# A two-layer encoder trunk: GpSimd left idle in the first pair, the shift earlier, and layer norm as two VectorE operations

## The chip, the cores and the metric

The kernel runs on one core of a Trainium2 chip. The metric is the device time of one execution in microseconds (us), as a median over runs. The engines are named as in the profile: PE is TensorE's matmul and PEld its weight load, DVE is VectorE, ACT is ScalarE, POOL is GpSimd, SP is SyncE, which here issues most of the DMAs. Each engine works through its own queue in order and waits on semaphores for the others.

## The reference

Two groups of tokens, p (1024 tokens) and s (512), go through the same two layers of width 1024. Cut to what matters here:

```python
for l in range(2):
    mod = silu(c) @ w_mod[l] + b_mod[l]
    shift, scale, gate = split(mod, 3)
    u = x * (1 + scale) + shift
    y = mixer_a(u, w_in_a, w_out_a) if l == 0 else mixer_b(u, w_in_b, w_out_b, sink_b)
    x = layernorm(ALPHA * x + gate * y, ln_g[l], ln_b[l])
# layernorm(h) = (h - mean) * rsqrt(var + 1e-5) * g + b, over the 1024 columns
```

mixer_a projects u to q, k and v for three dilations (1, 4 and 16) and to a gate z, runs windowed attention for each dilation, merges them and multiplies by w_out. mixer_b is windowed attention with grouped keys. All inputs and results are float32.

## The kernel before

*Accuracy and chunks.* A float32 product is made of three faster ones. Every operand is split into hi (a rounded copy, type fp32r) and lo (operand minus hi), and each step over 128 rows of the contraction is three matmuls: hi of the weight with hi of u, hi with lo, lo with hi. With eight such steps a group of 512 columns is 24 matmuls (`run_plan`, L370, into the PSUM tiles `a`, of which there are two). The work is a list of chunks, each with one or two weight tiles of 128x1024, one or more groups and an evacuation of the PSUM tile (L160 on ScalarE, L162 on VectorE).

*Order.* The program is written out in the order in which each engine shall work; nothing is reordered later. While a group's matmuls are written, `slot()` is called after every four of them (eight where they have 256 columns) and after each evacuation. `after(n, f)` writes the work of f at the n-th slot from there, `spread(tasks, slots)` lets a list of tasks follow slot by slot, with None for an empty slot, and `hook(i, f)` writes f ahead of chunk i. A slot later in the program is a place later in every queue that f uses.

*Weights.* `w_load` (L316) brings a tile from DRAM on SP's queue, two tiles ahead. `w_split` makes hi and lo of the next tile. The chunk's `how` says where: "pool" makes both on GpSimd (hi in two halves, L336; lo in four quarters, L346), "act" makes hi on ScalarE (L338) and lo on GpSimd, "fast" makes hi on ScalarE and lo in one operation on VectorE. Buffers in SBUF are 45 slabs of 128x1024 words, given and returned by hand.

*The start.* The first layer for s comes first. A pair is the work of two heads; the first pair's chunks 0 to 3 make q4, k4, q16 and k16, chunk 4 the values of dilations 4 and 16 (four groups of 24 matmuls with 256 columns). x of s is transposed into xT (L1346). Of the three parts of `mod`, scale is computed first (`mod_mm`, L206, then `mod_tr`: L212, L218, L220, and L227/L228 on VectorE), so chunks 0 to 3 can start on u without shift: `u_scaled` makes hi on ScalarE (L1315) and lo on VectorE (L1316). The shift is computed between them, from the weights `mods[1]` (eight loads). Then `whole` makes u with shift (`u_whole`: the sum for even k on ScalarE, L1325, for odd k on VectorE, L1321; hi at L1326 and L1322; lo on GpSimd, L1327, and VectorE, L1323), and `swap` puts it in place ahead of chunk 4 (EARLY is 4). What chunks 0 to 3 lack, `early_bias` adds: VectorE accumulates shift times the weight over k (`acc`, L1295 and L1297, 16 operations for two weight tiles), TensorE sums over the partitions with ones (L1304), and VectorE adds the column to Q4, K4, Q16 and K16 (L1306, L1309). The first scores are L578.

*Out layers and layer norm.* After both groups' attention, w_out is applied in 12 blocks of 128 tokens, each of two groups of 24 matmuls; this happens once in each layer. A block's evacuation on VectorE multiplies by the gate (L1093, tile ystg), adds ALPHA x (L1094) and takes the statistics of the half (L1095). Then follow, by slots: `stat` (mean and variance on VectorE, L1105; on GpSimd minus the mean, plus eps, to the power -0.5, and their product, L1106 to L1109), four slots after it `norm` on ScalarE (L1113, x times rstd minus mean times rstd), two later `scale` (times g, L1117), three later `shift` (plus b, L1121), and the store (L1123, SP). Of each block one of scale and shift is on VectorE and the other on GpSimd, alternating by block. The last block of all is done in halves at once (`finish_last`). Other work shares the engines there: L736, L794, L804 and L805 merge the last attention results, L787 reads back their factors f_p, L1069 and L1070 split the next block's input, L275 and L278 transpose x of s for the second layer, whose first steps are L946 and L949.

Of the kernel before, what the change touches and what calls it, by code (L numbers as in the profile page):

```python
# [75 lines left out]
def trunk(ctx: ExitStack, tc: tile.TileContext, x_p, x_s, c_p, c_s, w_mod, b_mod, ln_g, ln_b,  # L76
# [248 lines left out]
    def w_split():  # L325
        i = ahead[1]
        if i < len(loads):
            ahead[1] += 1
            t = raw_t.pop(i)
            hi = slabs.get(F32R, t.shape)  # L330
            lo = slabs.get(F32R, t.shape)
            how = loads[i][1]
            k = t.shape[1]
            if how == "pool":
                for ks in (slice(0, k // 2), slice(k // 2, k)):
                        nc.gpsimd.tensor_scalar(hi[:, ks], t[:, ks], 1.0, 1.0, ALU.mult, ALU.mult)  # L336
            else:
                nc.scalar.activation(hi, t, AF.Copy)  # L338
            if i == 0:
                for k in (0, 4):  # L340
                    nc.gpsimd.tensor_tensor(lo[:, k:k + 4], t[:, k:k + 4], hi[:, k:k + 4].bitcast(F32), ALU.subtract)
            else:
                n = 1 if how == "fast" else 4
                f = lambda a, j: a.rearrange("p k c -> p (k c)")[:, D // n * j:D // n * (j + 1)]
                for j in range(n):
                    (nc.vector if how == "fast" else nc.gpsimd).tensor_tensor(  # L346
                        f(lo, j), f(t, j), f(hi, j).bitcast(F32), ALU.subtract)
            if i < EARLY:
                early[i] = t
            else:  # L350
                slabs.put(t)
            w_t[i] = (hi, lo)
            w_fetch()
# [467 lines left out]
    def layer_a(r, half=None, done=None, use=None):  # L821
# [6 lines left out]
        for p in range(NP):  # L828
# [86 lines left out]
            if early_p:  # L915
# [3 lines left out]
                  how="act" if r == "s" else "pool")  # L919
# [126 lines left out]
    class Block:  # L1046
# [54 lines left out]
        def stat(self):  # L1101
            P = nc.gpsimd
            self.mv = mv = wk.tile([128, 2], F32, tag="mv", name="mv", bufs=4)
            self.nm = nm = wk.tile([128, 1], F32, tag="nmr", name="nmr", bufs=4)
# [3 lines left out]
            P.tensor_tensor(mv[:, 1:2], mv[:, 1:2], mhalf, ALU.pow)  # L1108
            P.tensor_tensor(nm, nm, mv[:, 1:2], ALU.mult)  # L1109

        def norm(self, cs=slice(0, D)):
            x = self.x[:, cs]
            nc.scalar.activation(x, x, AF.Identity, bias=self.nm, scale=self.mv[:, 1:2])  # L1113

        def scale(self, engine, cs=slice(0, D)):
            x = self.x[:, cs]
            engine.tensor_tensor(x, x, ROW["g"][:, cs], ALU.mult)  # L1117

        def shift(self, engine, cs=slice(0, D)):
            x = self.x[:, cs]  # L1120
            engine.tensor_tensor(x, x, ROW["b"][:, cs], ALU.add)  # L1121
# [6 lines left out]
        def finish(self):  # L1128

            V, P = nc.vector, nc.gpsimd  # L1130
            e = (V, P) if self.b % 2 else (P, V)
            keep = (self.r, self.l) == ("s", 0)
            return [self.stat, None, None, None, self.norm, None, lambda: self.scale(e[0]), None, None,
                    lambda: self.shift(e[1])] + ([] if keep else [self.free])

        def finish_last(self):
            V, P = nc.vector, nc.gpsimd
            self.stat()
            parts = [slice(0, 512), slice(512, 1024)]
            for cs in parts:  # L1140
                self.norm(cs)
            for cs in parts:
                self.scale(V, cs)
                self.shift(V, cs)
            self.free()

    def out_layer(l, first, p0):
# [22 lines left out]
        def then(j):  # L1170
            def f():
# [11 lines left out]
                t = [None] * (8 if j == 0 else 1) + t  # L1183
# [24 lines left out]
    with tc.manual_schedule():  # L1208
# [109 lines left out]
        def u_whole(k, t, m, u):  # L1318
            hi, lo = u[:, 0], u[:, 1]
            if k % 2:  # L1320
                nc.vector.tensor_scalar(t, t, m[:, 8 + k:9 + k], m[:, k:k + 1], ALU.mult, ALU.add)  # L1321
                nc.vector.tensor_copy(hi, t)  # L1322
                nc.vector.tensor_tensor(lo, t, hi.bitcast(F32), ALU.subtract)  # L1323
            else:
                nc.scalar.activation(t, t, AF.Identity, bias=m[:, k:k + 1], scale=m[:, 8 + k:9 + k])  # L1325
                nc.scalar.activation(hi, t, AF.Copy)  # L1326
                nc.gpsimd.tensor_tensor(lo, t, hi.bitcast(F32), ALU.subtract)  # L1327
# [37 lines left out]
        def whole():  # L1365
            for k in range(NK):
                new.append(slabs.get(F32R, (128, 2, 512)))
                u_whole(k, xk[k], m, new[k])
            slabs.put(*xT)
# [47 lines left out]
```

## Time and profile before

| | us |
|---|---|
| median of 3 runs | 2642.94 |
| lowest and highest | 2630.94, 2643.33 |
| the profiled execution | 2628.36 |
| its span, first to last instruction | 2626.3 |
| mean granted TensorE clock | 0.992 of full |

The profile is of one execution, so its numbers are summed against 2628.36 and not against the median. In its tables a row of a stage gives the busy time of each engine with the number of instructions in brackets, then PEclk (the granted TensorE clock as a share of full speed), the DMA engines' busy share and GB/s. In the timeline a row gives start and duration, engine, source line, operation, tiles written and read with their shapes, the number of instructions joined, and in square brackets the idle time of that engine before it with what ended it. Idle time of an engine that nothing waits for costs nothing.

### The profile page before, as it was taken

What the parts mean: (1) busy time and instruction counts of PE and PEld (TensorE: products, weight loads), DVE (VectorE), ACT (ScalarE), POOL (GpSimd) and SP (SyncE); (2) the same over time, 40 slices, a digit from 0 to 9 for tenths busy, and PEclk for the clock granted to TensorE, in tenths of its full rate; (3) what the DMA queues carried; (4) which work ended last, traced back from release to release, by engine and by line L of the source; (5) the groups of instructions that cost most, each with busy time, mean ns of one, the idle gap of its engine ahead of it and who ended that gap; (6) DMA issues with size and microseconds to landing.
All of it is one profiled execution on the core that took longest, in us unless ns stands there. A gap on an engine that the chain in (4) does not pass through costs nothing.

```text
span 2626.3 us, 39811 instructions
## 1 busy us (share of the span) xinstructions
PE 2565.7 (98%) x15139; PEld 2117.3 (81%) x15139; DVE 1114.8 (42%) x2602; ACT 981.8 (37%) x2327; POOL 1073.3 (41%) x1495
## 2 busy tenths in 40 slices
PE   7999999999999999999999999998999999999998
PEld 5777778888888888888888888887787778888786
DVE  4533333333243424333333434245654553454666
ACT  3344345643142424233232424232326643444421
POOL 5343444445323424332324233226546752233633
PEclk9999999999999999999999999999999999999999
DMA  8454543333222212132323232225442320112453
GB/s 283 122 136 143 154 100 106 101 101 91 61 58 70 68 48 67 41 81 58 81 51 79 49 81 58 61 68 172 158 155 66 101 85 25 49 49 65 137 176 112
DMA packets 294678, 247.38 MB, mean 94 GB/s; under 512 B 29656, under 2 KB 257880, under 8 KB 294488
## 3 DMA queue, kind: packets, MB, share of 16 engines
q1 hardware_dynamic: 291160, 244.35, 32.8%
q8 instruction: 119, 1.95, 0.3%
q10 hardware_dynamic: 3328, 0.49, 0.1%
q14 instruction: 71, 0.58, 0.1%
HBM read 198.16 MB, written 25.67 MB: 85 GB/s over the span
## 4 chain that ended last, share of the span: by engine, by line
PE 72%; DVE 2%; ACT 1%; POOL 1%; DMA 1%; issue 1%; SPq 0%; POOLq 0%; DVEq 0%; ACTq 0%
PE a L370 56%; PE o L475 5%; PE t L434 5%; PE s L573 2%; PE s L574 2%; PE s L578 1%; POOL s L269 0%; PE t L591 0%; DMA s<-g_s 0%; DVE s L1094 0%; ACT P L423 0%; ACT ustg L278 0%; DMA s<-s 0%; DVE s L1121 0%; DMA s<-in_x_sample_dram 0%
## 5 line engine op out<-in xcount | busy, mean ns | idle before, releaser
L370 PE MATMUL a<-s,s 128*128 128x512 f32 (+1 forms) x9648 | 2113.0, 369 | 14.0 <-DVE ystg L1093 5.2
L370 PEld LDWEIGHTS a<-s,s 128*128 128x128 f32 x9648 | 1613.7, 190 | 294.5 <-issue 16.5
L346 POOL TENSOR_TENSOR s<-s,s 128x256 fp32r<-128x256 f32 x844 | 618.9, 767 | 469.6 <-PE a L370 203.1
L423 ACT ACTIVATE P<-P,st 128x256 f32<-128x256 f32 (+2 forms) x576 | 312.5, 543 | 559.3 <-DVE st L417 557.6
L417 DVE CUSTOM_DVE_ANT_0 P<-s,bias 128x256 f32<-128x256 f32 (+2 forms) x576 | 251.5, 473 | 270.9 <-PE s L578 130.0
L336 POOL TENSOR_SCALAR s<-s 128x512 fp32r<-128x512 f32 x278 | 171.2, 635 | 408.9 <-PE a L370 346.0
L444 DVE COPY PT<-t 128x256 f32<-128x256 f32 (+3 forms) x320 | 141.4, 449 | 170.1 <-PE t L434 166.5
L736 POOL TENSOR_TENSOR s<-s,s 128x256 f32<-128x256 f32 x92 | 66.7, 753 | 339.0 <-DMA s<-f_p 282.8
L434 PE MATMUL t<-ident,P 128*128 128x128 f32 x1408 | 201.2, 273 | 0.8 <-ACT PT L442 0.8
L434 PEld LDWEIGHTS t<-ident,P 128*128 128x128 f32 x1408 | 168.6, 139 | 29.4 <-ACT PT L442 1.2
L549 DVE TENSOR_TENSOR s<-a,s 64x512 fp32r<-64x512 f32 x128 | 110.0, 860 | 164.1 <-ACT s L547 163.1
L475 PE MATMUL o<-PT,s 128*64 128x256 f32 (+1 forms) x1984 | 178.7, 324 | 0.0
L442 ACT ACTIVATE PT<-t 128x256 f32<-128x256 f32 (+3 forms) x320 | 126.6, 400 | 127.6 <-PE t L434 125.5
L475 PEld LDWEIGHTS o<-PT,s 128*64 128x64 f32 x1984 | 119.1, 136 | 64.7 <-issue 33.8
L573 PE MATMUL s<-s,s 128*128 128x256 f32 (+2 forms) x512 | 144.9, 299 | 10.3 <-DVE st L417 10.2
L574 PE MATMUL s<-s,s 128*128 128x256 f32 (+2 forms) x512 | 143.5, 297 | 2.5 <-DMA s<-s 2.5
L162 DVE COPY s<-a 128x128 f32<-128x128 f32 (+2 forms) x113 | 53.5, 492 | 213.3 <-PE a L370 200.2
L558 DVE TENSOR_TENSOR s<-a,s 64x512 fp32r<-64x512 f32 x80 | 77.5, 969 | 143.9 <-ACT s L556 142.9
L160 ACT ACTIVATE s<-a 128x128 f32<-128x128 f32 (+2 forms) x139 | 52.9, 409 | 224.4 <-PE a L370 224.4
L573 PEld LDWEIGHTS s<-s,s 128*128 128x128 f32 x512 | 97.1, 190 | 25.2 <-DVE st L417 15.8
L547 ACT ACTIVATE s<-a 64x512 fp32r<-64x512 f32 x128 | 100.2, 783 | 25.6 <-PE a L370 24.8
L584 DVE SCALAR_TENSOR_TENSOR s<-th,a 128x512 f32<-128x512 f32 x48 | 43.1, 899 | 151.9 <-ACT th L582 151.9
(112 smaller groups left out, 1573.5 us busy)
## 6 DMA issues: line engine op xcount, KB each, us to landing
s<-in_w_in_a_dram SPq DMA_DIRECT2D x128, 512.0 KB, 5.3
s<-in_w_mod_dram SPq DMA_DIRECT2D x48, 512.0 KB, 7.9
s<-in_w_in_b_dram SPq DMA_DIRECT2D x40, 512.0 KB, 5.2
s<-in_w_in_a_dram SPq DMA_DIRECT2D x64, 256.0 KB, 3.3
s<-s SPq DMA_DIRECT2D x64, 256.0 KB, 5.2
s<-f_p SPq DMA_DIRECT2D x48, 256.0 KB, 5.1
s<-in_x_prompt_dram SPq DMA_DIRECT2D x16, 512.0 KB, 4.2
g_p<-s SPq DMA_DIRECT2D x16, 512.0 KB, 2.6
```

What stands on the lines that cost most here:

```text
L336: nc.gpsimd.tensor_scalar(hi[:, ks], t[:, ks], 1.0, 1.0, ALU.mult, ALU.mult)
L346: (nc.vector if how == "fast" else nc.gpsimd).tensor_tensor(f(lo, j), f(t, j), f(hi, j).bitcast(F32), ALU.subtract)
L370: nc.tensor.matmul(a, lhsT=lhsT, rhs=rhs, start=(n == 0), stop=(n == 3 * NK - 1))
L417: nc.vector.tensor_tensor_reduce(out=p[:, :s.n], in0=t[:, :s.n], in1=s.bias(h), op0=ALU.add, op1=ALU.min, scale=-0.125, scalar=3e38, accum ...
L423: nc.scalar.activation(p[:, :s.n], p[:, :s.n], AF.Exp, scale=-1.0, bias=s.st[:, s.b, h, 0:1], accum_out=s.st[:, s.b, h, 1:2])
L434: nc.tensor.transpose(t[0:r0 + n, i, :], s.P[h][:, c0 - r0:c0 + n], ident)
L442: nc.scalar.activation(pt[r0:r0 + n, i:j], t[r0:r0 + n, i:j], AF.Copy)
L444: nc.vector.tensor_copy(pt[r0:r0 + n, i:j], t[r0:r0 + n, i:j])
L475: nc.tensor.matmul(o[64 * h:64 * h + 64, cs], lhsT=v(h)[r0:r0 + n, :], rhs=pair.PT[h][r0:r0 + n, blocks, :], start=fresh[steps[0]], stop=stop)
L549: nc.vector.tensor_tensor(w[e][me[1 - e]], f[e](a[me[e]]), w[e][me[e]].bitcast(F32), ALU.subtract)
L573: nc.tensor.matmul(t, lhsT=q, rhs=kk, start=True, stop=False)
L574: nc.tensor.matmul(t, lhsT=q, rhs=kl, start=False, stop=True)
```

## The change

It has two parts.

*The first pair.* Every weight tile of the first pair is split "fast", and the very first one in two halves, hi on ScalarE and lo on VectorE; GpSimd is left with the bias tiles of the attention (L510) there. All eight loads of the shift's weights are issued ahead of weight tiles 2 and 3, where five of them came behind tile 2 on SP's queue. The shift is multiplied at slot 8 instead of 13, transposed at slot 10 instead of 15. `whole` becomes five tasks at slots 11, 13, 15, 17 and 19 (it was one at slot 16): task j makes the sums for two k (one on ScalarE, one on VectorE) and both hi's on ScalarE, and the lo's follow on VectorE at the start of the next task. The bias correction starts at slot 17 for the first two tiles and 25 for the other two (24 and 28 before).

*Layer norm.* `norm` is gone, and `scale` and `shift` are one operation each, always on VectorE: (x - mean) * g, then that times rstd plus b. GpSimd keeps two small operations, plus eps and the power. Scale stands six empty slots after `stat`, shift two slots after scale; the first block's list starts after seven empty slots instead of eight.

```diff
@@ w_split
-            if how == "pool":
-                for ks in (slice(0, k // 2), slice(k // 2, k)):
+            if i == 0:
+                for ks in (slice(0, 4), slice(4, 8)):
+                    nc.scalar.activation(hi[:, ks], t[:, ks], AF.Copy)
+                    nc.vector.tensor_tensor(lo[:, ks], t[:, ks], hi[:, ks].bitcast(F32), ALU.subtract)
+            else:
+                if how == "pool":
+                    for ks in (slice(0, k // 2), slice(k // 2, k)):
                         nc.gpsimd.tensor_scalar(hi[:, ks], t[:, ks], 1.0, 1.0, ALU.mult, ALU.mult)
-            else:
-                nc.scalar.activation(hi, t, AF.Copy)
-            if i == 0:
-                for k in (0, 4):
-                    nc.gpsimd.tensor_tensor(lo[:, k:k + 4], t[:, k:k + 4], hi[:, k:k + 4].bitcast(F32), ALU.subtract)
-            else:
+                else:
+                    nc.scalar.activation(hi, t, AF.Copy)
                 n = 1 if how == "fast" else 4
@@ the layer's chunks, twice
-                          how="act" if r == "s" and (p or kind == "q4") else "pool")
+                          how="fast" if early_p else "act" if r == "s" else "pool")
...
@@ Block
-            P.tensor_scalar(nm, mv[:, 0:1], -1.0, 1.0, ALU.mult, ALU.mult)
             P.tensor_scalar(mv[:, 1:2], mv[:, 1:2], EPS, None, ALU.add)
             P.tensor_tensor(mv[:, 1:2], mv[:, 1:2], mhalf, ALU.pow)
-            P.tensor_tensor(nm, nm, mv[:, 1:2], ALU.mult)
-
-        def norm(self, cs=slice(0, D)):
-            nc.scalar.activation(x, x, AF.Identity, bias=self.nm, scale=self.mv[:, 1:2])
-        def scale(self, engine, cs=slice(0, D)):
-            engine.tensor_tensor(x, x, ROW["g"][:, cs], ALU.mult)
-        def shift(self, engine, cs=slice(0, D)):
-            engine.tensor_tensor(x, x, ROW["b"][:, cs], ALU.add)
+        def scale(self, cs=slice(0, D)):
+            nc.vector.scalar_tensor_tensor(x, x, self.mv[:, 0:1], ROW["g"][:, cs], ALU.subtract, ALU.mult)
+        def shift(self, cs=slice(0, D)):
+            nc.vector.scalar_tensor_tensor(x, x, self.mv[:, 1:2], ROW["b"][:, cs], ALU.mult, ALU.add)
...
-            return [self.stat, None, None, None, self.norm, None, lambda: self.scale(e[0]), None, None,
-                    lambda: self.shift(e[1])] + ([] if keep else [self.free])
+            return [self.stat] + [None] * 6 + [self.scale, None, self.shift] + ([] if keep else [self.free])
...
@@ the start
-        for k in range(3):
-            mods[1].append(load_mod(0, 0, k))
+        mods[1] = [load_mod(0, 0, k) for k in range(NK)]
         mod_tr(0, 1, mod_mm(mods[0]))
         w_split()
-        for k in range(3, NK):
-            mods[1].append(load_mod(0, 0, k))
...
+        def whole(j):
+            while lows:
+                lows.pop(0)()
+            if j == 0:
+                new.extend(slabs.get(F32R, (128, 2, 512)) for _ in range(NK))
+            if j == 4:
+                slabs.put(*xT)
+                return
+            for k in (2 * j, 2 * j + 1):
+                whole_sum(k, xk[k], m)
+            for k in (2 * j, 2 * j + 1):
+                lows.append(whole_parts(k, xk[k], new[k]))
...
-        after(13, shift)
-        after(15, lambda: mod_tr(0, 0, box["m"]))
-        after(16, whole)
+        after(8, shift)
+        after(10, lambda: mod_tr(0, 0, box["m"]))
+        for j in range(5):
+            after(11 + 2 * j, lambda j=j: whole(j))
...
-                    after(24 + 4 * i + j, f)
+                    after(17 + 8 * i + j, f)
```

Lines of the changed kernel are numbered a little differently: L338 becomes L343, L370 L371, L1093 L1094, L794 L795, L1117 L1111, L1121 L1115, L1304 L1291, L1297 L1284.

How the queues move at the places that matter. ScalarE at the start, from the evacuation of chunk 0 to the first sum of u with shift, before (s_5 and s_8 are the hi parts of the two weight tiles of chunk 4; modrow and modcol are the shift on its way):

```order
L160 ACTIVATE s_41_338<-a 128x512
L338 ACTIVATE s_5_400<-s_1_360 128x1024
L212 ACTIVATE modrow<-t 128x512
L338 ACTIVATE s_8_454<-s_4_379 128x1024
L220 ACTIVATE modcol<-t 128x512
L1325 ACTIVATE s_15_199<-s_15_199,modT_94 128x512
L1326 ACTIVATE s_11_482<-s_15_199 128x512
```

and after (s_38, s_44 and s_2 are hi of weight tiles 1, 2 and 3, s_5 of tile 4):

```order
L343 ACTIVATE s_38_329<-s_14_180 128x1024
L343 ACTIVATE s_44_349<-s_29_303 128x1024
L343 ACTIVATE s_2_364<-s_40_333 128x1024
L160 ACTIVATE s_41_335<-a 128x512
L212 ACTIVATE modrow<-t 128x512
L343 ACTIVATE s_5_408<-s_1_353 128x1024
L220 ACTIVATE modcol<-t 128x512
L1309 ACTIVATE s_15_199<-s_15_199,modT_94 128x512
L1312 ACTIVATE s_8_437<-s_15_199 128x512
```

Three weight splits now stand ahead of chunk 0's evacuation and of modrow. On TensorE the first correction matmul stood inside chunk 4's third group before; after, it stands between chunk 3's last matmul (512 columns) and chunk 4's first (256):

```order
L371 MATMUL a<-s_37_312,s_2_364 128x512 x2
L371 MATMUL a<-s_37_312,s_3_365 128x512
L1291 MATMUL t<-ones,acc 128x1 x2
L371 MATMUL a<-s_5_408,s_8_437 128x256 x2
L371 MATMUL a<-s_6_409,s_8_437 128x256
```

Before, in that third group:

```order
L370 MATMUL a<-s_5_400,s_22_490 128x256 x2
L1304 MATMUL t<-ones,acc 128x1 x2
L370 MATMUL a<-s_6_401,s_22_490 128x256
L370 MATMUL a<-s_5_400,s_23_494 128x256 x2
L370 MATMUL a<-s_6_401,s_23_494 128x256
```

So the whole of chunk 4 now stands behind that matmul; the second correction matmul moves from chunk 4's fourth group to its third, behind 64 matmuls of the chunk. VectorE in the first out layer, around the merge L794 at 1830.6 us, before:

```order
L1094 SCALAR_TENSOR_TENSOR s_18_16737<-s_18_16737,ystg 128x512
L1095 BN_STATS s_16918<-s_18_16737 128x6
L1117 TENSOR_TENSOR s_37_16482<-s_37_16482,s_28_16840 128x1024
L794 TENSOR_TENSOR s_22_16931<-s_38_15895,s_22_16931 128x1024
L1121 TENSOR_TENSOR s_21_16465<-s_21_16465,s_26_16842 128x1024
L1093 TENSOR_TENSOR ystg<-a,s_30_16467 128x512
```

and after:

```order
L1095 SCALAR_TENSOR_TENSOR s_16_16704<-s_16_16704,ystg 128x512
L1096 BN_STATS s_16878<-s_16_16704 128x6
L1111 SCALAR_TENSOR_TENSOR s_24_16432<-s_24_16432,mv,s_38_16807 128x1024
L1111 SCALAR_TENSOR_TENSOR s_35_16449<-s_35_16449,mv,s_38_16807 128x1024
L795 TENSOR_TENSOR s_10_16890<-s_27_15862,s_10_16890 128x1024
L1115 SCALAR_TENSOR_TENSOR s_24_16432<-s_24_16432,mv,s_26_16809 128x1024
L1115 SCALAR_TENSOR_TENSOR s_35_16449<-s_35_16449,mv,s_26_16809 128x1024
L1094 TENSOR_TENSOR ystg<-a,s_2_16434 128x512
```

The two blocks' layer norms meet here: two scales now stand ahead of the merge and two shifts between it and the next evacuation, where one of each stood.

More of the change, by code (lines that the diff above doesn't have):

```diff
@@ L918, in layer_a @@
                   [proj_v(r, 0, 128 * b, v23_group(st, S, b)) for b in range(nb)], pre=None if early_p else alloc23,
-                  how="act" if r == "s" else "pool")
+                  how="fast" if early_p else "act" if r == "s" else "pool")
             if not early_p:
@@ L1103, in stat @@
             self.mv = mv = wk.tile([128, 2], F32, tag="mv", name="mv", bufs=4)
-            self.nm = nm = wk.tile([128, 1], F32, tag="nmr", name="nmr", bufs=4)
             nc.vector.bn_aggr(mv, self.s6)
-            P.tensor_scalar(nm, mv[:, 0:1], -1.0, 1.0, ALU.mult, ALU.mult)
             P.tensor_scalar(mv[:, 1:2], mv[:, 1:2], EPS, None, ALU.add)
             P.tensor_tensor(mv[:, 1:2], mv[:, 1:2], mhalf, ALU.pow)
-            P.tensor_tensor(nm, nm, mv[:, 1:2], ALU.mult)
-        def norm(self, cs=slice(0, D)):
+        def scale(self, cs=slice(0, D)):
             x = self.x[:, cs]
-            nc.scalar.activation(x, x, AF.Identity, bias=self.nm, scale=self.mv[:, 1:2])
-        def scale(self, engine, cs=slice(0, D)):
+            nc.vector.scalar_tensor_tensor(x, x, self.mv[:, 0:1], ROW["g"][:, cs], ALU.subtract, ALU.mult)
+        def shift(self, cs=slice(0, D)):
             x = self.x[:, cs]
-            engine.tensor_tensor(x, x, ROW["g"][:, cs], ALU.mult)
-        def shift(self, engine, cs=slice(0, D)):
-            x = self.x[:, cs]
-            engine.tensor_tensor(x, x, ROW["b"][:, cs], ALU.add)
+            nc.vector.scalar_tensor_tensor(x, x, self.mv[:, 1:2], ROW["b"][:, cs], ALU.mult, ALU.add)
             out = y_out[self.r] if self.l else x_in[self.r, 1]
@@ L1128, in finish @@
         def finish(self):
-            V, P = nc.vector, nc.gpsimd
-            e = (V, P) if self.b % 2 else (P, V)
             keep = (self.r, self.l) == ("s", 0)
-            return [self.stat, None, None, None, self.norm, None, lambda: self.scale(e[0]), None, None,
-                    lambda: self.shift(e[1])] + ([] if keep else [self.free])
+            return [self.stat] + [None] * 6 + [self.scale, None, self.shift] + ([] if keep else [self.free])
         def finish_last(self):
-            V, P = nc.vector, nc.gpsimd
             self.stat()
[L1139 to L1144, printed above, removed]
+            for cs in (slice(0, 512), slice(512, 1024)):
+                self.scale(cs)
+                self.shift(cs)
             self.free()
@@ L1182, in f @@
                     t.append(lambda: [b.free() for b in blocks[:4]])
-                t = [None] * (8 if j == 0 else 1) + t
+                t = [None] * (7 if j == 0 else 1) + t
                 spread(t, len(t))
@@ L1316, in u_scaled, with whole_sum, whole_parts @@
             nc.vector.scalar_tensor_tensor(lo, t, m[:, 8 + k:9 + k], hi.bitcast(F32), ALU.mult, ALU.subtract)
-        def u_whole(k, t, m, u):
-            hi, lo = u[:, 0], u[:, 1]
+        def whole_sum(k, t, m):
             if k % 2:
                 nc.vector.tensor_scalar(t, t, m[:, 8 + k:9 + k], m[:, k:k + 1], ALU.mult, ALU.add)
-                nc.vector.tensor_copy(hi, t)
-                nc.vector.tensor_tensor(lo, t, hi.bitcast(F32), ALU.subtract)
             else:
                 nc.scalar.activation(t, t, AF.Identity, bias=m[:, k:k + 1], scale=m[:, 8 + k:9 + k])
-                nc.scalar.activation(hi, t, AF.Copy)
-                nc.gpsimd.tensor_tensor(lo, t, hi.bitcast(F32), ALU.subtract)
+        def whole_parts(k, t, u):
+            nc.scalar.activation(u[:, 0], t, AF.Copy)
+            return lambda: nc.vector.tensor_tensor(u[:, 1], t, u[:, 0].bitcast(F32), ALU.subtract)
         rows = load_c()
@@ L1363, in trunk @@
         new = []
[L1365 to L1369, printed above, removed]
+        lows = []
+        def whole(j):
[10 more added lines that the diff above has]
+                lows.append(whole_parts(k, xk[k], new[k]))
         def swap():
```

## The prediction

> **What bounds the kernel now.** I read the page's engine shares first, then TensorE's list of waits, then tables by stage, then the timeline at the two places that the change touches.
>
> ```profile
> span 2626.3 us, 39811 instructions
> PE 2565.7 (98%) x15139; PEld 2117.3 (81%) x15139; DVE 1114.8 (42%) x2602; ACT 981.8 (37%) x2327; POOL 1073.3 (41%) x1495
> ```
>
> TensorE is busy for 2565.7 of 2626.3 us. The change takes no matmul away, so it can win only two things: part of the 60.6 us in which TensorE idles, and time that TensorE spends at half clock, which counts as busy. TensorE's waits (total, times, longest):
>
> ```profile
> PE s L573 <- DVE st L417: 10.2, 10, 2.3
> PE t L1304 <- DVE acc L1297: 6.1, 3, 4.5
> PE a L370 <- DVE ystg L1093: 5.2, 2, 3.7
> PE a L370 <- DVE s L949: 1.3, 1, 1.3
> PE t L275 <- POOL s L1121: 1.1, 1, 1.1
> ```
>
> The first row belongs to softmax and is not touched. The second is the bias correction of the first pair; the third and fifth are the layer norm's, in the first out layer; the fourth follows it directly. Together these four are 13.7 us. What the waits do to the clock is in the table by stage (us, busy PE, PEld, DVE, ACT, POOL, then PEclk, the granted clock):
>
> ```profile
> 26.90:33.70 6.80, 5.99 (x13) 4.30 (x14) 6.80 (x7) 3.72 (x7) 6.72 (x7) 0.50 1.06 378
> 57.20:64.40 7.20, 4.87 (x29) 3.75 (x29) 6.94 (x9) 0.72 (x2) 7.04 (x9) 1.00 0.72 213
> 64.40:67.80 3.40, 3.40 (x19) 3.40 (x18) 3.40 (x6) 0.00 (x0) 3.40 (x7) 0.50 1.13 317
> 67.80:74.70 6.90, 2.07 (x16) 1.78 (x15) 6.90 (x12) 0.00 (x0) 6.74 (x12) 0.99 0.72 234
> 1791.60:1795.00 3.40, 3.33 (x11) 2.83 (x12) 1.56 (x9) 2.45 (x9) 3.40 (x7) 0.50 1.17 282
> 1832.50:1835.90 3.40, 0.86 (x4) 0.38 (x2) 3.40 (x2) 0.00 (x0) 2.79 (x1) 1.00 0.00 0
> 1835.90:1842.70 6.80, 5.67 (x13) 4.46 (x14) 5.83 (x9) 1.15 (x2) 0.80 (x3) 0.50 0.81 295
> 1876.90:1880.30 3.40, 1.85 (x8) 1.22 (x7) 3.33 (x4) 0.00 (x0) 0.63 (x1) 1.00 0.26 104
> 1889.80:1900.70 10.90, 10.90 (x49) 9.01 (x48) 7.62 (x11) 2.31 (x2) 5.47 (x6) 1.00 0.65 193
> ```
>
> In the first pair VectorE and GpSimd are both busy nearly all the time and TensorE is not. After an idle slice the next stretch of 3.4 or 6.8 us runs at 0.50, in which half of the stretch is lost work: 1.7 us for each 3.4. The 2.3 us wait of softmax (first row of the waits) is followed by such a stretch at 1791.6; the wait that ends in 1876.9:1880.3 (1.55 idle, row below) is not.
>
> **The first pair.** Its rows before, in order of time (start, duration):
>
> ```profile
> 26.36 9.54 DVE L1316 SCALAR_TENSOR_TENSOR s<-s,modT,s 128x512 fp32r<-128x512 f32 x8 [0.90 <-ACT s L1315]
> 36.73 0.60 ACT L160 ACTIVATE s<-a 128x512 f32<-128x512 f32 x1 [6.11 <-PE a L370]
> 40.08 1.21 POOL L336 TENSOR_SCALAR s<-s 128x512 fp32r<-128x512 f32 x2 [0.33 <-DMA s<-in_w_in_a_dram]
> 41.80 1.06 ACT L338 ACTIVATE s<-s 128x1024 fp32r<-128x1024 f32 x1 [4.47 <-DMA s<-in_w_in_a_dram]
> 51.34 0.82 ACT L1325 ACTIVATE s<-s,modT 128x512 f32<-128x512 f32 x1 [1.55 <-DVE modT L227]
> 51.45 0.54 DVE L1321 TENSOR_SCALAR s<-s,modT 128x512 f32<-128x512 f32 x1
> 52.49 0.69 DVE L1323 TENSOR_TENSOR s<-s,s 128x512 fp32r<-128x512 f32 x1
> 57.59 0.62 PE L370 MATMUL a<-s,s 128*128 128x256 f32 x3 [0.28 <-ACT s L160]
> 65.16 9.41 DVE L1297 SCALAR_TENSOR_TENSOR acc<-s,modT,acc 128x128 f32<-128x128 f32 x14
> 73.89 0.38 PE L1304 MATMUL t<-ones,acc 128*128 128x1 f32 x2 [4.49 <-DVE acc L1297]
> 79.47 1.13 DVE L1297 SCALAR_TENSOR_TENSOR acc<-s,modT,acc 128x128 f32<-128x128 f32 x4
> 85.90 0.71 PE L578 MATMUL s<-s 64*128 64x128 f32 x8
> 1955.84 6.37 PE L370 MATMUL a<-s,s 128*128 128x256 f32 x51 [0.47 <-ACT s L160]
> ```
>
> Chunks 0 to 3 (24 matmuls each, on u without shift). *Chunk 0.* Eight lo parts of u take 9.54 us beside GpSimd's splits, 1.19 each; the like subtraction alone takes 0.69 (52.49), so without GpSimd they pass in 5.5. But VectorE now also makes the lo of w0, two of 0.69, and TensorE still falls to half clock here, as in 26.90:33.70 before. I let chunk 0 end at about 35 instead of 36.5. *Shift.* Its multiplication moves five slots earlier, into chunk 1. On ScalarE the copies modrow and modcol stand behind the hi parts of w2, w3 and w4, and on VectorE L227 behind their lo parts. w3 lands at 40.0 and w4 at 41.7 (the starts of 40.08 and 41.80, which waited for them); hi of w3 1.06, the evacuation 0.60, modrow 0.60 give 42.3; w4's hi and lo end at 43.4 and 44.6 (1.06, then 1.21 for a subtraction of 128x1024, row 1824.57 below); four small operations more, and the shift is there at 45.3, six us earlier than at 51.3. TensorE waits up to 1.5 us for modrow there. Chunk 3 ends at about 56 instead of 57.2: **minus 1.2**, bounds 0 (w3 lands later, one for one) and minus 2.5.
>
> *VectorE's queue up to the first correction matmul.* From 45.3: four sums of 0.54 (51.45), eight lo parts of 0.69, an evacuation of 0.69, one lo of a weight at 1.21, 16 accumulations. These took 0.67 each beside GpSimd (9.41 for 14) and 0.28 when GpSimd stood still (1.13 for 4). I take 0.28, because the changed order gives GpSimd nothing at this place: 2.2 + 5.5 + 0.7 + 1.2 + 4.5 = 14.1, so 59.4 at the least; with the waits for ScalarE's sums and hi parts, which alternate with it, about 61. L1304 (L1291 of the changed kernel) now stands ahead of chunk 4's first matmul, so TensorE waits from 56 to 61: a new wait of 5 us in the place of the 4.5, and one half-clock stretch after it, 1.7. *Chunk 4.* 96 matmuls at 0.125 (6.37 for 51) are 12.0. The second correction's 16 accumulations pass in VectorE's queue behind two weight lo's and an evacuation: 61 + 3.1 + 1.1 (the first correction added to Q4 and K4, an estimate from two sums of 0.54) + 4.5 = 69.7, and TensorE reaches their matmul after 64 matmuls and the slow stretch, at 61.2 + 8.0 + 1.7 = 70.9: no wait. Chunk 4 so ends at 61.2 + 12.0 + 1.7 + 0.5 = 75.4; before, it ended at 84.0 (eight matmuls of 0.23 ahead of the first scores at 85.90). **Minus 8.6 in all for the start** (the 1.2 are in it); bounds: minus 11 where the accumulations also fit between ScalarE's waits, minus 2.5 where they stay at 0.67 (16 times 0.39 later, at 67).
>
> Later in this pair the weights' hi go to ScalarE (1.06) and lo to VectorE (1.21) instead of GpSimd, beside softmax. TensorE's only wait from 84 to 200 us was
>
> ```profile
> PE s L574 <- DMA s<-s: 2.5, 1, 2.5
> ```
>
> so neither engine held it up there, and one or two such pieces per weight must first use up that slack. I take 0; bounds 0 and plus 2.3, one wait like softmax's longest.
>
> **Layer norm.** Rows before, first out layer, then the tail:
>
> ```profile
> 1824.57 1.21 DVE L1117 TENSOR_TENSOR s<-s,s 128x1024 f32<-128x1024 f32 x1
> 1830.64 2.49 DVE L794 TENSOR_TENSOR s<-s,s 128x1024 f32<-128x1024 f32 x1 [4.87 <-DMA s<-f_p]
> 1833.06 3.31 DVE L1121 TENSOR_TENSOR s<-s,s 128x1024 f32<-128x1024 f32 x1
> 1837.03 20.22 PE L370 MATMUL a<-s,s 128*128 128x512 f32 x76 [3.67 <-DVE ystg L1093]
> 1879.27 25.91 PE L370 MATMUL a<-s,s 128*128 128x512 f32 x113 [1.55 <-DVE ystg L1093]
> 2618.66 0.57 POOL L1108 TENSOR_TENSOR mv<-mv,mhalf 128x1 f32<-128x1 f32 x1
> 2622.43 0.69 DVE L1121 TENSOR_TENSOR s<-s,s 128x512 f32<-128x512 f32 x1
> 2589.08 2.41 POOL L1117 TENSOR_TENSOR s<-s,s 128x1024 f32<-128x1024 f32 x1 [1.36 <-ACT s L1113]
> 2589.14 2.89 DVE L1094 SCALAR_TENSOR_TENSOR s<-s,ystg 128x512 f32<-128x512 f32 x1
> 2594.58 0.69 DVE L1094 SCALAR_TENSOR_TENSOR s<-s,ystg 128x512 f32<-128x512 f32 x1
> ```
>
> The trace has no SCALAR_TENSOR_TENSOR of 128x1024. At 128x512 it takes 0.69 alone (2594.58), as TENSOR_TENSOR does (2622.43), so I take the 1.21 of the larger TENSOR_TENSOR; the other end is the 2.89 that one took beside GpSimd. *At 1833.* Two new scale operations stand ahead of L794 and fit into the 4.87 us that it waits for its DMA. L794 begins at 1830.6; GpSimd's L1121 no longer runs beside it, so it ends at about 1832.2; two shifts of 1.21 end at 1834.6, and L1093 (0.69) at 1835.3. TensorE, idle since 1833.36 (1837.03 less 3.67), waits 1.9 instead of 3.67: **minus 1.8**. The 6.8 us at half clock behind it cost 3.4. An idle 1.55 kept the clock and 2.3 lost it; 1.9 lies about midway. I let it keep the clock: **minus 3.4**, bounds 0 and minus 3.4. *At 1858 and 1879* TensorE waits for GpSimd's shift (1.1) and for a shift of VectorE that waited for GpSimd's scale (1.55); neither operation exists now: **minus 2.6**, bounds 0 and minus 2.6. *Behind the last block* L949 waits on ScalarE, which loses its norm: **minus 0.5**, bounds 0 and minus 1.3. *Steady blocks:* one operation moves from GpSimd to VectorE, 7.62 + 1.21 = 8.8 of 10.9 us, TensorE still the longest: 0. *Tail.* Before, rstd is there at 2619.2 and the last shift ends at 2623.1. Now the first scale needs only the mean and runs beside eps and pow, of which one small operation ahead is gone: rstd at 2619.0, then shift, scale, shift at 0.69 end at 2621.1: **minus 2.0**, bounds minus 1.3 and minus 2.3. Out layer 1 had no wait that the change removes: 0. The gate_p load that now follows a second store on SP's queue is wanted a block later: 0.
>
> **Sum.** 8.6 + 1.8 + 3.4 + 2.6 + 0.5 + 2.0 = 18.9 less. The profiled execution took 2628.36 us (2.1 beyond its span), so 2609.5 by its own measure. It lies 14.6 below the median of 2642.94 and below the fastest run shown, 2630.94; the trace says nothing about that part, so I carry it: 2642.9 - 18.9 = **2624**.
>
> **Two rules weighed.** The row 64.40:67.80 shows half clock behind a slice with idle time, and 2.3 us was enough once. The Trainium skill ("TensorE: Matmul & The Clock Gate", What's actually happening) asks for at least one whole idle window of about 3.4 us; the dip at 1791.6 differs from that. By the rule a wait of 1.9 us could never cost the clock and the 3.4 would be sure; by the rows alone the sum lies between 15.5 and 18.9. Second, L1094 took 2.89 beside GpSimd's 2.41 and 0.69 alone. The Trainium skill ("SBUF — State Buffer", Who interferes with whom) has a VectorE instruction with two SBUF inputs locked out for the whole of a GpSimd instruction that reads SBUF; the trace agrees. By it, the accumulations at 0.28 are the rule and minus 8.6 stands; it also speaks against the layer norm's two new operations wherever GpSimd still splits weights.
>
> **Rivals.** *(A) VectorE is the bound at the start whatever GpSimd does.* All of GpSimd's splitting comes to VectorE's queue; if accumulations and lo parts stay near 0.67 and 1.19, the correction matmul waits until 67 and beyond and the start gives 2.5. With 1833 still over the clock's limit the rest gives 6.9: 9.4 in all, 2633.5. For it: VectorE busy 6.90 of 6.90 us in 67.80:74.70; against it the 1.13 for 4. *(B) The clock takes the gain back:* a second slow stretch at the start (1.7), the one at 1833 stays (3.4) and w3 lands two us late: 18.9 - 7.1 = 11.8, 2631. *(C) Slower: the layer norm makes VectorE the bound in the out layers.* A steady block has 7.62 us of VectorE, of which 1.21 go and 2x come; beyond x = 2.25 the block exceeds 10.9. Over 24 blocks, 24 (2x - 4.49) eats the 18.9 at x = 2.64 and makes the kernel 13 us slower at x = 2.9, 2656. The contended 2.89 shows that such a price exists; against it, most of the GpSimd work that contended (scale and shift, 2.41 each) is itself removed.
>
> **How the numbers follow.** My sum, between 13 and 24 less, 0.62; A 0.22; B 0.11; C 0.05. A change under 0.5% (13 us) is about what a measurement here cannot tell from none. Faster: 0.62 and a little of B, 0.64; same: A and the rest of B, 0.31; slower: 0.05. The range goes from 2606 (24 less, on the run of 2630.94) to 2637 (6 less on the median), which takes in A and B.
>
> **What would show it.** In the profile after: GpSimd idle from 26 to 75; accumulations at 0.28; one wait of about 5 us on the correction ahead of chunk 4; first scores near 77; no 0.50 at 1836's place; no wait on GpSimd's layer norm; the first layer norm operation at 1.2 us. I am wrong if accumulations stay above 0.5, if shift is not there by 47, or if L1111 takes above 2.

## The result, and the profile after

| | before | changed |
|---|---|---|
| median of 7 runs, us | 2642.94 | 2623.13 |
| lowest and highest | 2630.94, 2653.64 | 2607.99, 2625.16 |
| the profiled execution | 2628.36 | 2624.83 |

The ratio is 0.9925 with a 95% interval of 0.9905 to 0.9945: 19.8 us less in the median, clear of no change, against 18.9 forecast. But the two profiled executions differ by only 3.5. The page after begins:

```profile
span 2622.9 us, 39659 instructions
PE 2560.3 (98%) x15139; PEld 2116.9 (81%) x15139; DVE 1131.4 (43%) x2636; ACT 961.5 (37%) x2314; POOL 960.9 (37%) x1368
```

GpSimd lost 112 us of work, and VectorE gained only 17. TensorE's waits after (in all, times, longest):

```profile
PE s L574 <- DVE st L418: 21.9, 9, 13.4
PE s L575 <- DMA s<-s: 4.8, 3, 4.0
PE t L1291 <- DVE acc L1284: 3.9, 1, 3.9
PE a L371 <- DVE ystg L1094: 3.1, 1, 3.1
```

The correction's wait is one of 3.9 where it was three with 6.1; the waits of the out layer on GpSimd and on the second shift are gone, the one at 1833 is 3.1 where it was 3.7. What is new stands in the first row: softmax, which the change does not touch, waits once for 13.4 us, where its longest wait before was 2.3. VectorE and GpSimd around it, in the trace after (four more GpSimd rows of the same two kinds stand where the dots are):

```profile
1782.36 13.67 DVE L1095 SCALAR_TENSOR_TENSOR s<-s,ystg 128x512 f32<-128x512 f32 x1
1780.96 2.82 POOL L347 TENSOR_TENSOR s<-s,s 128x256 fp32r<-128x256 f32 x4
1783.76 1.20 POOL L341 TENSOR_SCALAR s<-s 128x512 fp32r<-128x512 f32 x2
...
1792.73 2.76 POOL L347 TENSOR_TENSOR s<-s,s 128x256 fp32r<-128x256 f32 x4
```

The evacuation's ALPHA x + y, 0.69 us in the median, lasts 13.67: from 1782.36 until 0.54 after 1795.49, when GpSimd's last split of w_out ends. Not one row of GpSimd has idle time before it, and each starts where the one before it ends. In the trace before, the same operation at the same place took 1.78, and there it is a GpSimd row that is longer than 1.2:

```profile
1788.78 1.78 DVE L1094 SCALAR_TENSOR_TENSOR s<-s,ystg 128x512 f32<-128x512 f32 x1
1789.98 1.64 POOL L336 TENSOR_SCALAR s<-s 128x512 fp32r<-128x512 f32 x2
```

So the execution profiled before was one without this block and the one profiled after had it. Taking TensorE's instructions in order, the changed kernel is 9.9 us ahead behind the first pair's correction, 5.6 ahead before this operation, 5.5 behind after it, and 2.0 ahead at the last matmul. Of the 4.3 us lost between 85 and 1782 us, 2.7 go near 185: there a wait for a DMA lasts 4.0 us and half clock 6.8, where before they lasted 2.5 and 3.4. The pair of kernels with y in PSUM, further down, shows no such loss at this place (9.2 us ahead in front of it, 10.1 at it), so it is not laid to the change.

The start, answering to the rows of before:

```profile
25.22 1.29 DVE L337 TENSOR_TENSOR s<-s,s 128x512 fp32r<-128x512 f32 x2
26.43 5.38 DVE L1303 SCALAR_TENSOR_TENSOR s<-s,modT,s 128x512 fp32r<-128x512 f32 x8
44.77 0.82 ACT L1309 ACTIVATE s<-s,modT 128x512 f32<-128x512 f32 x1 [0.81 <-DVE modT L227]
57.89 2.19 DVE L1284 SCALAR_TENSOR_TENSOR acc<-s,modT,acc 128x128 f32<-128x128 f32 x8
59.96 0.70 PE L1291 MATMUL t<-ones,acc 128*128 128x1 f32 x4 [3.93 <-DVE acc L1284]
75.87 0.71 PE L579 MATMUL s<-s 64*128 64x128 f32 x8
```

Eight lo parts take 5.38 instead of 9.54, the shift is there at 44.8 instead of 51.3, accumulations take 0.27 each (2.19 for eight, which overlap a little), and the first scores come at 75.87 instead of 85.90. The out layer's critical place and the tail:

```profile
1830.32 2.47 DVE L1111 SCALAR_TENSOR_TENSOR s<-s,mv,s 128x1024 f32<-128x1024 f32 x2
1834.51 2.83 POOL L737 TENSOR_TENSOR s<-s,s 128x256 f32<-128x256 f32 x4 [6.66 <-DMA s<-f_p]
1836.61 2.52 DVE L795 TENSOR_TENSOR s<-s,s 128x1024 f32<-128x1024 f32 x1 [3.83 <-DMA s<-f_p]
1839.06 2.46 DVE L1115 SCALAR_TENSOR_TENSOR s<-s,mv,s 128x1024 f32<-128x1024 f32 x2
1842.17 4.07 PE L371 MATMUL a<-s,s 128*128 128x512 f32 x10 [3.06 <-DVE ystg L1094]
2616.05 0.77 POOL L1106 TENSOR_SCALAR mv<-mv 128x1 f32<-128x1 f32 x1 [10.01 <-DVE mv L1105]
2618.95 0.75 DVE L1115 SCALAR_TENSOR_TENSOR s<-s,mv,s 128x512 f32<-128x512 f32 x1
```

The two new operations cost 1.23 each, as taken. L795 still takes 2.5, the two shifts follow it, and TensorE waits 3.06 and then runs at half clock (the window from 1842.2 on):

```profile
1842.20:1845.60 3.40, 3.40 (x8) 2.70 (x9) 3.33 (x4) 0.00 (x0) 0.00 (x0) 0.53 0.97 320
```

### The profile page after: what moved, and what is told of

Read it like the earlier page. It is cut to its first block, busy times and chain, and to the rows that moved or that the text cites. A ratio compares the mean times of both kernels' runs of the same rounds, so it can differ in the third digit from the quotient of the medians.

```text
span 2622.9 us, 39659 instructions
## 1 busy us (share of the span) xinstructions
PE 2560.3 (98%) x15139; PEld 2116.9 (81%) x15139; DVE 1131.4 (43%) x2636; ACT 961.5 (37%) x2314; POOL 960.9 (37%) x1368
## 4 chain that ended last, share of the span: by engine, by line
PE 73%; DVE 2%; DMA 1%; issue 1%; ACT 1%; POOL 1%; SPq 0%; POOLq 0%; DVEq 0%
PE a L371 56%; PE o L476 5%; PE t L435 5%; PE s L574 2%; PE s L575 2%; PE s L579 1%; DVE s L1095 1%; POOL s L347 1%; PE t L592 0%; DMA s<-g_s 0%; PE t L275 0%; ACT P L424 0%; DMA s<-in_x_sample_dram 0%; DMA s<-s 0%; POOL s L341 0%
## 5 line engine op out<-in xcount | busy, mean ns | idle before, releaser
L371 PE MATMUL a<-s,s 128*128 128x512 f32 (+1 forms) x9648 | 2107.8, 369 | 6.9 <-DVE ystg L1094 3.1
L371 PEld LDWEIGHTS a<-s,s 128*128 128x128 f32 x9648 | 1612.4, 190 | 282.2 <-issue 15.3
L347 POOL TENSOR_TENSOR s<-s,s 128x256 fp32r<-128x256 f32 x808 | 591.2, 765 | 486.1 <-PE a L371 202.5
L341 POOL TENSOR_SCALAR s<-s 128x512 fp32r<-128x512 f32 x264 | 160.5, 627 | 408.7 <-PE a L371 345.6
L737 POOL TENSOR_TENSOR s<-s,s 128x256 f32<-128x256 f32 x92 | 66.8, 754 | 343.0 <-DMA s<-f_p 286.8
```

Of the source, the lines that this page charges most:

```text
L347: (nc.vector if how == "fast" else nc.gpsimd).tensor_tensor(f(lo, j), f(t, j), f(hi, j).bitcast(F32), ALU.subtract)
L371: nc.tensor.matmul(a, lhsT=lhsT, rhs=rhs, start=(n == 0), stop=(n == 3 * NK - 1))
```

## The experiments

The rows of the locked operation gave two questions. Theory: VectorE's operation with two operands in SBUF is locked out while GpSimd works without a gap (called the lock from here on); that makes some executions of both kernels some 14 us longer, and it is the 14.6 that I carried unexplained. Rival: the scatter comes from transfers. And where in the change is the gain? The runs were made on three chips, each beside the kernel before, whose medians there were 2638.46, 2637.99 and 2639.43.

**The parts alone, on the kernel before.** The first takes only the first pair's part of the change, the second only the layer norm's:

```diff
 # e1_start: w_split, how=, mods[1], whole, early_bias as changed; Block as before
-        after(16, whole)
+        for j in range(5):
+            after(11 + 2 * j, lambda j=j: whole(j))
```

> The kernel before with the first pair's part of the change alone (splits, earlier shift, u in tasks, earlier correction); layer norm as before. My sum gave 8.6 us less for this part, and the profile after has the first scores 10.0 us earlier. Theory (the parts add, and a separate lock of VectorE by GpSimd in the first out layer, there in both kernels, makes some executions 10 to 15 us longer): first scores at 76, a median 8 to 11 below the kernel before on this chip, and executions still scattered over some 15 us. Rival (the gain is not the start's, but the accident of which executions were locked): under 4 us.

```diff
 # e2_ln: Block and out_layer as changed; the rest as before
-            return [self.stat, None, None, None, self.norm, ...
+            return [self.stat] + [None] * 6 + [self.scale, None, self.shift] + ...
```

> The kernel before with the layer norm's part alone. My sum gave 10.3 us less: 1.8 and 3.4 at 1833, 2.6 at 1858 and 1879, 0.5, and 2.0 at the tail. The profile after still shows 3.1 us of wait and some half clock at that place, so I now expect 6 to 8 less, with the waits at 1858 and 1879 gone and L1111 and L1115 at 1.2 to 1.3 us each. Executions scattered as before. Rival (two-input operations on VectorE are locked out by GpSimd as often as the old ones): 0 to 3 less.

Measured against 24 runs of the kernel before (median 2638.46, 2625.21 to 2649.75): 2629.61 (ratio 0.9986, 0.9965 to 1.0006) and 2621.54 (0.9950, 0.9929 to 0.9971). The medians fall by 8.8 and 16.9, which would make 25.7, more than the 19.8 of the whole change; the second is outside what I expected. By its interval the first cannot be told from no change, so this run does not decide between its theory and its rival. Executions ran from 2616.58 to 2639.99 and from 2615.85 to 2634.96, so a median here depends on how many were locked. The waits came as expected: first scores early in the one, none for GpSimd's layer norm in the other. Both profiled executions were locked at the same place, in the second:

```profile
1788.12 13.56 DVE L1094 SCALAR_TENSOR_TENSOR s<-s,ystg 128x512 f32<-128x512 f32 x1
```

The 24 runs of the kernel before themselves stand in groups: six from 2625 to 2629, sixteen from 2635 to 2643, two at 2649. The medians of the first two groups are 11.8 apart.

**One operand out of SBUF.** y goes back to the PSUM tile, in the changed kernel and in the kernel before:

```diff
-                y = wk.tile([128, 512], F32, tag="stg", name="ystg")
-                nc.vector.tensor_tensor(y, a, ROW["gate" + self.r][:, cs], ALU.mult)
-                nc.vector.scalar_tensor_tensor(x, x, ALPHA, y, ALU.mult, ALU.add)
+                nc.vector.tensor_tensor(a, a, ROW["gate" + self.r][:, cs], ALU.mult)
+                nc.vector.scalar_tensor_tensor(x, x, ALPHA, a, ALU.mult, ALU.add)
```

> The changed kernel, with y = a * gate written back to PSUM instead of to an SBUF tile, so that ALPHA x + y reads one operand from SBUF and one from PSUM. Theory (lock): in the profile after, that operation took 13.67 us because GpSimd worked through 20 split instructions without a gap; with one SBUF operand it takes 0.69 everywhere, the softmax wait of 13.4 us and the half clock behind it cannot come, and the executions close up at the fast end, 2604 to 2612, median near 2609, some 14 below the changed kernel. It holds the PSUM tile 0.7 us longer, up to 1 us in all. Rival (the scatter comes from transfers from DRAM, which also differ between the two profiles): median 2618 to 2626, still scattered over 10 us or more.

> The kernel before with the same edit of y. Theory (lock): the executions close up near the profiled 2628, at 2624 to 2632, where the kernel before has 2631 to 2654; so 12 to 16 less in the median without any of the change. Rival (scatter from transfers): median 2638 to 2645, scattered as before.

Measured: 2604.62 (2601.10 to 2606.37) and 2621.23 (2618.75 to 2623.51). Both close up to some 5 us, 18.5 and 17.2 us below the same kernels with y in SBUF. The operation in the changed kernel, with y in SBUF and then in PSUM (ns, least, median and most of 48):

```profile
L1095 DVE SCALAR_TENSOR_TENSOR s<-s,ystg x48: 691/692/13673, 1782.4 to 2614.3; 128x512 f32<-128x512 f32 x48
```

```profile
L1094 DVE SCALAR_TENSOR_TENSOR s<-s,a x48: 686/687/690, 1778.8 to 2594.0; 128x512 f32<-128x512 f32 x48
```

The theory holds and the rival falls. Both came out 4 to 7 us lower than I expected; the shorter locks, of up to 3.9 us in the two profiles, are gone too and may account for it. Without the lock's scatter the change is worth 2621.23 - 2604.62 = 16.6 us. The next runs stand on this base.

**Gaps for GpSimd.** The changed kernel with y in SBUF as it is, and hi of both out layers' weights on ScalarE:

```diff
-        chunk(tiles(0), ..., pre=begin, keep=W, deep=3)
-        chunk(tiles(1), ..., pre=second, keep=W, deep=-1)
+        chunk(tiles(0), ..., pre=begin, keep=W, deep=3, how="act")
+        chunk(tiles(1), ..., pre=second, keep=W, deep=-1, how="act")
```

> The changed kernel as it is (y in SBUF), but hi of the first w_out's eight tiles and the second's on ScalarE; GpSimd keeps only the lo parts, 2.8 us a tile, each behind a hi of ScalarE. Theory (VectorE is locked out for as long as GpSimd's instructions follow one another without a gap): with gaps between the tiles the operation at 1782 takes at most about 3.5 us, the 13.4 us wait does not come, and executions close up at 2606 to 2614. Rival (what matters is two operands in SBUF while GpSimd has work queued, gaps or not): an operation of 8 us or more there in the profile, executions scattered to 2620 and beyond.

Measured: 2603.61 (2601.94 to 2606.49), 0.9871 of the kernel before (0.9835 to 0.9908), 2.4 below what I expected. The same operation now takes at most 1.1:

```profile
L1095 DVE SCALAR_TENSOR_TENSOR s<-s,ystg x48: 691/693/1107, 1780.0 to 2594.5; 128x512 f32<-128x512 f32 x48
```

So the long lock is gone with y still in SBUF, and of theory and rival the theory stands. The edit does two things at once, though: it makes gaps in GpSimd's stream and takes its hi operations out of it. And at 1780.0 the operation passed in 0.69 while four lo parts of GpSimd ran (from 1779.41, for 3.28), so it did not need a gap there; what is shown is that none of the five executions was long.

**What GpSimd's stillness is worth at the start.** y in PSUM, all of the change, but the first pair's weights split as before (the very first tile stays in two halves on ScalarE and VectorE):

```diff
-                          how="fast" if early_p else "act" if r == "s" else "pool")
+                          how="act" if r == "s" and (p or kind == "q4") else "pool")
 # and, for the values' tiles
-                  how="fast" if early_p else "act" if r == "s" else "pool")
+                  how="act" if r == "s" else "pool")
```

> The changed kernel with y in PSUM, the first pair's weights split as in the kernel before (hi and lo of tiles 1 to 3 and of later ones on GpSimd, tile 4 and the values' tiles with lo on GpSimd); the shift stays at its earlier place and u is still made on ScalarE and VectorE. Theory (GpSimd's stillness is what makes VectorE fast there): accumulations take 0.6 to 0.7 us instead of 0.28, the correction's wait grows to 8 to 12 us, first scores 4 to 7 us later than 75.2, median 2608 to 2612. Rival (the earlier shift alone is the gain; VectorE, relieved of weight lo parts, is as quick beside GpSimd): within 2 us of 2604.6.

Measured: 2613.78 (2609.94 to 2616.33), 9.2 above 2604.62 and 1.8 above what I expected at the most. The accumulations (again least, median, most) and the wait:

```profile
L1283 DVE SCALAR_TENSOR_TENSOR acc<-s,modT,acc x28: 333/692/826, 56.9 to 77.7; 128x128 f32<-128x128 f32 x28
```

```profile
67.54 1.11 PE L1290 MATMUL t<-ones,acc 128*128 128x1 f32 x4 [10.99 <-DVE acc L1283]
84.64 0.72 PE L579 MATMUL s<-s 64*128 64x128 f32 x8
```

In the changed kernel the same list reads 346/347/349. First scores are at 84.6, nearly the 85.9 of before, though the shift came 5 us early; that is some 8 us later than with GpSimd still, a little more than I expected. The theory holds: GpSimd's stillness is what makes VectorE fast here.

**The layer norm alone, without the lock.** The kernel before with y in PSUM and the second part:

```diff
 # e8_ln_psum: the edit of e2_ln and that of e3_psum together, on the kernel before
```

> The kernel before with y in PSUM and the layer norm's part of the change alone. The two traces with y in PSUM give 10.1 to 10.7 for the start, 1.0 against the change at 1833, 1.8 at 1858, 2.1 at 1879, 1.5 behind the last block, 1.4 at the tail: 5.9 to 6.5 for the layer norm in all. Theory (the parts add): 2621.2 less 6 to 7, so 2614 to 2615.5. Rival (they overlap, or layer norm's gain was the lock's): 2618 or more.

Measured: 2613.82 (2611.96 to 2618.09): 7.4 less than 2621.23. That is about what I expected, so the rival, that this gain was the lock's, falls. The other 9.2 of the 16.6 are the start's part by subtraction; the start's part alone with y in PSUM was not run. And 2613.82 with no part of the start's change is the same as the 2613.78 above with all of it but GpSimd's stillness: without that, the earlier shift, the tasks and the earlier correction together brought nothing that can be measured within executions 6 us apart. What each of them would bring alone is not shown.

**The correction later.** y in PSUM, and the correction matmuls six slots later:

```diff
-            return [lambda k=k: acc(k) for k in range(0, NK, 2)] + [None] * 3 + [add]
+            return [lambda k=k: acc(k) for k in range(0, NK, 2)] + [None] * 9 + [add]
```

> The changed kernel with y in PSUM, and each correction matmul six slots later, inside chunk 4, its accumulations where they were. Theory (VectorE's queue is the bound of this stretch, and the correction only the place where it shows): the wait of 4.2 us on the correction goes, but a new one of 2 to 4 us comes in chunk 4's second group, which needs the PSUM tile that VectorE evacuates behind two weight lo parts at 62.3; the first scores move by under 2 us, the median by under 2 from 2604.6. Rival (the correction's place is the bound): first scores 4 to 6 us earlier, 2599 to 2600.

Measured: 2600.51 (2600.18 to 2602.40), 4.1 less. My theory falls: the wait is gone, and no new one came.

```profile
61.39 0.68 DVE L162 COPY s<-a 128x512 f32<-128x512 f32 x1
62.36 3.12 PE L371 MATMUL a<-s,s 128*128 128x256 f32 x24
71.20 0.49 PE L579 MATMUL s<-s 64*128 64x128 f32 x4
```

It is chunk 4's third group, at 62.4, that follows VectorE's evacuation at 61.4 and not the second, which started at 59.0 behind an evacuation of ScalarE. VectorE's queue had just enough slack; the correction's place was the bound.

**The shifts at 1833.** y in PSUM, and shift two slots later, then in another run directly behind scale:

```diff
-            return [self.stat] + [None] * 6 + [self.scale, None, self.shift] + ...
+            return [self.stat] + [None] * 6 + [self.scale, None, None, None, self.shift] + ...   # e5_shift_late
+            return [self.stat] + [None] * 6 + [self.scale, self.shift] + ...                     # e10_shift_early
```

> The changed kernel with y in PSUM, and the layer norm's shift two slots later, which puts both L1115 of the first two blocks behind the next evacuation on VectorE. Theory (the 3.4 us wait at that place is made by the two shifts that stand ahead of the evacuation): the wait falls by their 2.5 us to about 0.9 and the clock is kept: 2.5 + 1.7 less than the kernel with y in PSUM (2604.6), so 2599 to 2602. Rival (the merge that waits for the read-back of f_p sets it, and the shifts only fill the time): within 1 us of 2604.6.

> The changed kernel with y in PSUM, and the layer norm's shift directly behind scale, so that both L1114 of the first two blocks stand ahead of the merge L795, where VectorE idles 3.4 us for the read-back of f_p. Theory (that stretch is VectorE's work, and only what fits into the idle time ahead of the merge is free): the wait falls from 3.4 to about 1, no new wait behind it, the clock is kept; 2.5 + 1.7 less than 2604.6, 2599 to 2602. Rival (the idle time is needed, or the clock drops anyway): within 1.5 of 2604.6.

Measured: 2609.99 (2608.18 to 2613.16), slower by 5.4, and 2600.47 (2599.57 to 2602.62), 4.2 faster. With the late shift the wait fell as expected, to 1.04, and the clock stayed; but one evacuation later the same work is in the way, so neither what I expected nor its rival came:

```profile
1822.15 5.74 PE L371 MATMUL a<-s,s 128*128 128x512 f32 x24 [1.04 <-DVE s L1094]
1825.85 2.48 DVE L1114 SCALAR_TENSOR_TENSOR s<-s,mv,s 128x1024 f32<-128x1024 f32 x2
1830.88 15.48 PE L371 MATMUL a<-s,s 128*128 128x512 f32 x60 [2.99 <-DVE s L1094]
```

VectorE is busy for 16.14 of the 17 us from 1820 to 1837 there. Its profiled execution lies 3.0 behind that of the base at the last matmul; the rest of the 5.4 is not explained. With the early shift, both fit into the time in which VectorE waits for f_p:

```profile
1813.85 2.48 DVE L1114 SCALAR_TENSOR_TENSOR s<-s,mv,s 128x1024 f32<-128x1024 f32 x2
1817.29 2.14 DVE L795 TENSOR_TENSOR s<-s,s 128x1024 f32<-128x1024 f32 x1 [0.96 <-DMA s<-f_p]
```

**All three edits.** y in PSUM, later correction, early shift:

```diff
 # e11_both: the edits of e3_psum, e6_acc_late and e10_shift_early on the changed kernel
```

> The three edits together on the changed kernel: y in PSUM, the correction matmuls six slots later, shift directly behind scale. If they add: 2600.5 less 4, so 2595 to 2598; if the out layer's gain is given back, 2599 to 2601.

Measured: 2599.89 (2597.54 to 2600.36), 0.9855 of the kernel before (0.9824 to 0.9887): faster than both kernels, but they do not add. Against the kernel with the later correction its trace is 2.0 behind at 185 us already and level at the end. Of TensorE's waits in that first stretch only the one on s<-s differs, 3.2 against 2.9; most of the rest is the clock, at half for 6.8 us there and for 3.4 in the other. By 1824 us it is 2.4 ahead. Of that it loses 1.2 in a new wait of 1.16 at 1826.6, and 1.6 at 2125, where it runs at half clock behind a wait of 1.90 and the other keeps its clock behind one of 1.72 (the later correction first, then all three edits; the clock is the third figure from the end):

```profile
2124.90:2128.30 3.40, 1.95 (x9) 1.62 (x10) 1.91 (x7) 2.85 (x6) 0.05 (x1) 1.00 0.20 77
```

```profile
2125.00:2128.40 3.40, 3.40 (x9) 2.72 (x10) 2.07 (x4) 1.50 (x4) 0.00 (x0) 0.51 0.21 78
```

Only the new wait lies beside the early shift. In these two executions the clock elsewhere takes most of its gain back; whether it does so in the others, whose medians differ by 0.6, is left open.

## Why the prediction came out right, and where it did not

*The whole:* 2624 forecast, 2623.13 measured. Part of this is luck. The 14.6 us by which the profiled execution lay below the median, which I carried without a reason, are by the evidence mostly the lock: y in PSUM takes 17.2 off the kernel before, and the traces of its two parts had one long operation each, of 13.66 and 13.56. No execution of the kernel before itself was profiled with the long lock. Judging by the groups, most executions of both kernels have it, so it stayed in the difference of the medians. Without it the change is worth 16.6, where the sum said 18.9: the start gave 0.6 more than its term and the layer norm 2.9 less, 7.4 where its terms sum to 10.3.

*The first pair, 8.6:* right, somewhat low. First scores came 10.0 earlier in the trace, and the part is worth 9.2 by subtraction. The shift came at 44.8 (45.3 forecast), accumulations 0.27 (0.28), chunk 4 at 60.5 (61.2), and the new wait 3.9 (5). The Trainium skill's rule ("SBUF — State Buffer", Who interferes with whom), that a VectorE instruction with two SBUF inputs contends with a GpSimd instruction that reads SBUF, under an exclusive lock, carried this step; the trace agrees, since the run with GpSimd's splits put back returned 0.69 an accumulation and 9.2 us. Rival A is thereby settled: VectorE is the bound only as long as GpSimd works beside it. What I had not separated is that the earlier shift, the tasks and the earlier correction bring nothing measurable without that stillness.

*At 1833, 1.8 and 3.4:* wrong, and the one step that failed. I wrote that L794 ends at 1832.2 since GpSimd's L1121 no longer runs beside it. It took 2.52 again. In both traces it ended 1.79 after GpSimd's merge L736 (L737), which also reads SBUF and was running when it began, and the change leaves that merge. It is a lock, and not an order that the program asks for: with the shift directly behind scale, L795 ended 1.24 before the merge, which then took 5.29 instead of 2.83. With two shifts behind L795 the wait was 3.06 instead of 1.9, and half clock came after all, for 3.4 us instead of 6.8. In order of instructions the change gains 1.3 us here of the 5.2 forecast; rival B's second item came half true. In the pairs of kernels with y in PSUM the place is even 2.3 to 2.7 us against the change, since the kernel before waits only 2.0 there and keeps its clock. The early shift shows the price: with the same two operations ahead of the merge on VectorE, the median is 4.2 lower.

*At 1858 and 1879, 2.6:* right, somewhat low; between the traces 1.5 and 1.8. *Behind the last block, 0.5:* the wait went, worth 1.5, above the bound of 1.3. *Tail, 2.0:* 1.4. GpSimd's small operation (plus eps) took 0.77 instead of 0.22, while VectorE's L1111 ran beside it: the lock works the other way round too. *Steady blocks, 0:* right; rival C did not come near, L1111 and L1115 have a median of 1.27 and 1.29.

*Two rules:* on the clock, I took 1.9 as lying between a wait of 1.55 that kept it and one of 2.3 that lost it. There is no such border in these traces. In the trace before, a wait of 2.01 lost it:

```profile
2148.61 0.27 PE L775 MATMUL t<-ident,f 128*8 128x128 f32 x1 [2.01 <-DVE f L768]
2150.00:2153.40 3.40, 3.40 (x10) 2.62 (x9) 2.69 (x4) 0.19 (x1) 0.00 (x0) 0.50 0.11 37
```

In the trace after, one of 1.58 that ended at 2489.9 lost it (0.51 from 2490.6 to 2494.0), and one of 2.22 that ended at 1775.1 kept it (1.00 from 1775.0 to 1782.0); with the first pair's weights split as before, one of 3.24 kept it:

```profile
1832.70 5.55 PE L371 MATMUL a<-s,s 128*128 128x512 f32 x23 [3.24 <-DVE s L1094]
1832.70:1836.10 3.40, 3.40 (x15) 2.78 (x16) 3.03 (x3) 0.25 (x2) 0.00 (x0) 1.00 0.73 254
```

So the length of a wait alone does not decide, and the 3.4 could not be forecast from it. The Trainium skill ("TensorE: Matmul & The Clock Gate", What's actually happening) asks for a whole idle window of about 3.4 us; the 1.58 and the 2.01 are far under that and were followed by half clock all the same.

## What to carry to other kernels

Where a VectorE operation reads two operands from SBUF, look at GpSimd's stream beside it: if that has no gap, the operation can wait for all of it, and here one PSUM operand removed the wait, and so did moving half of GpSimd's work elsewhere, which also left gaps in it. A kernel whose executions stand in groups more than 10 us apart, as here, may have such a place; look for it as the one long operation in a list of equal ones, before summing against one profiled execution. Work that goes to an engine costs nothing only in that engine's idle time: here it belonged ahead of the wait for a transfer, not behind it.

## What the runs showed of the hardware

A VectorE operation of 0.69 us waited 13.67 us for 20 GpSimd instructions in a row, each of which started as the one before ended. At the same place in the kernel before it slipped in after 1.78, beside a GpSimd stream that had no gap either; why it got in there is not shown. The Trainium skill ("SBUF — State Buffer", Who interferes with whom) calls the port pair that the two engines share an exclusive lock; here VectorE waited for a chain of GpSimd's instructions and not for one. GpSimd can be the one that waits: its merge of 2.83 took 5.29 beside L795 in the run with the early shift.
